# First modulation in float32 with its weights as stationary tiles, by quarters of rows; silu(c) broadcast once

## The chip, the cores and the metric

One core of a Trainium2 chip runs the whole program. The metric is the device time of one execution in microseconds, as the median of several. The engines are TensorE (PE; PEld is its load of stationary weights), VectorE (DVE), ScalarE (ACT), GpSimd (POOL) and SyncE (SP), whose queue issues nearly all transfers.

## The reference

Two blocks of a network run one behind the other; only the head of the first is touched. In layer 0, x (512 rows of 1024) and ctx (256 rows) are normalised, modulated by a vector that depends on c or c_ctx, and multiplied by w_in:

```python
mod_lat = (jax.nn.silu(c) @ w_ada[l] + b_ada[l])[:, None, :]
mod_ctx = jax.nn.silu(c_ctx) @ w_ada[l] + b_ada[l]
sh1, sc1, gt1, sh2, sc2, gt2 = jnp.split(mod_lat, 6, axis=-1)
csh1, csc1, cgt1, csh2, csc2, cgt2 = jnp.split(mod_ctx, 6, axis=-1)
h_lat = modulate(rms_norm(x_lat, g_mix[l]), sh1, sc1)   # h * (1 + scale) + shift
h_ctx = modulate(rms_norm(x_ctx, g_mix[l]), csh1, csc1)
z = h @ p['w_in']
```

The first modulation needs sh1 and sc1, the first two sixths of w_ada (1024 x 2048), for the two vectors c and c_ctx. The other four sixths are needed later in the layer, and all six again in layer 1.

## The kernel before

Activations lie with features on the partitions: 8 tiles of 128 features by 512 rows (x) and 256 rows (ctx). Large products keep float32 accuracy by splitting each operand into a rounded part and the rest (`hi`, `lo`; type float32r) and adding three products: hi by hi, hi by lo, lo by hi. `weights` does this for a weight tile of 128x1024: a copy on ScalarE (line 295) and a subtraction on VectorE or, where `pool` is set, GpSimd (line 296). `prods` issues the three matmuls of a product (line 425).

A scheduler orders the instructions of each engine by program order and by when its own model has their inputs ready; each engine then takes its instructions in that order. Tiles come from pools with a number of buffers a tag. The tag u6 has 18: the tiles of w_mod (`raw6`), the spare split weights and the split, modulated activations H all come from it. PSUM has two double banks (`psJ`) and four single ones (`psM`).

The head of `first_block` runs in this order. c and c_ctx are loaded as 16 columns (`cc`), silu is formed by a tanh and a product (lines 1344 and 1345; it leaves out the factor 0.5, which comes later), and split into `cparts`. x is loaded, then w_mod in 16 tiles of 512 KB. `stats` squares x on ScalarE (line 564), adds on VectorE, sums over partitions with a matmul by ones (line 571), takes the power -0.5 on GpSimd (line 343) and spreads the result with transposes (line 349). `modulation` runs twice, for half of the features each: for 8 k-tiles the weights are split, and the four columns of `cparts` are the stationary tile while 512 columns of weights stream (line 1382); the four rows of sums are copied out and transposed back to columns (line 1388), and lines 1395 to 1398 form shift and gain in `mods`. `second` then forms one tile of H: a scaled product on VectorE (line 1415), a rounded copy on ScalarE (line 1416), the rest on VectorE (line 1417). Three units of w_in, whose PSUM banks are kept, are multiplied in two halves of k; `silus` broadcasts silu(c) over the partitions with 16 transposes (line 555) and four copies (line 556), for the other sixths of w_ada, which VectorE multiplies (`ada_block`, line 532). Then the gates follow (`gates`), whose first matmul is of line 330. `silus` runs a second time behind the first layer's merge, since its buffers are used for other things meanwhile. `g_entry`, a product of two gains, is formed at the head in `consts` and used by `entry` for the second block.

Of the kernel before, what the change touches and what calls it, by code (L numbers as in the profile page):

```python
# [20 lines left out]
D = 1024  # L21
KD = 8
# [77 lines left out]
def _layout(inp):  # L100
# [6 lines left out]
    w = g["w_ada"][0][:, :2 * D].reshape(KD, 128, 2, 2, T)  # L107
    a["w_mod"] = np.ascontiguousarray(w.transpose(3, 0, 1, 2, 4)).reshape(2, KD, 128, 2 * T)
# [160 lines left out]
class Build:  # L269
# [782 lines left out]
    def attention(self, l, H, nq, gates, per):  # L1052
# [36 lines left out]
        for h in range(H_A):  # L1089
# [18 lines left out]
         "b0": (0.1, 0.3), "bl": (0.4, 1), "st": (0, 0, 1, 1, 2), "l": ({}, {"late": 2, "va": 0.5, "ai": 50, "aw": (0.3, 1), "bs": (0, 1), "bv": (0.1, 0.9), "bp": (0, 0.9), "bn": (0, 0.5), "as": (0, 0.7), "av": (0, 1), "ap": (0, 1)}), "ql": 0, "oa": (), "r2": ((0, 0), (1, 1)), "sg": 0, "lag": 4, "sc": (0.3, 0.8), "ve": 10, "vw": (0, 1), "bi": (29, 6, 0, 0, 0, 0, 0, 0, 0), "bw2": (0, 0.8), "mp": ((1, 2), (1, 5)), "up": (1, 1, 1), "fin": {3: (1, 1, 0), 4: (3, 1, 0), 5: (4, 2, 3), 6: (0, 1, 3), 10: (1, 1, 0)}, "pri": (0, 0, 0, 0, 0, 0, 0, 0, 200, 0, 0), "ns": (0, 0.8), "nv": (0, 1), "raw": (0, 1), "rpw": (0, 1)}  # L1108
# [230 lines left out]
    def first_block(self):  # L1339
# [4 lines left out]
        nc.scalar.activation(cc[:, 1], cc[:, 0], AF.Tanh, scale=0.5)  # L1344
        nc.vector.scalar_tensor_tensor(cc[:, 2], cc[:, 1], 1.0, cc[:, 0], op0=ALU.add, op1=ALU.mult)
# [14 lines left out]
        parts = self.cp.tile([128, KD, 2, 2], F32R, name="cparts")  # L1360
        c2 = cc[:, 2].rearrange("p (k c) -> p k c", c=2)
        nc.scalar.activation(parts[:, :, 0], c2, AF.Copy)
        nc.vector.tensor_sub(parts[:, :, 1], c2, parts[:, :, 0].bitcast(F32))
        norm, pre = {}, []
        W = self.W

        wmod = {}

        def fetch(half):
            for k in range(KD):  # L1370
                wmod[half, k] = raw6()
                nc.sync.dma_start(wmod[half, k], io["w_mod"][half, k])

        def modulation(half):

            ps = self.psJ()
            for k in range(KD):
# [11 lines left out]
            v = col[:, :32].rearrange("p (s m a c) -> p s m a c", s=2, m=4, a=2)  # L1389
            ms = slice(half * 4, half * 4 + 4)  # L1390
            out = mods[:, :, ms]
            b = self.col("b_ada0", 0, 16).rearrange("p (s m) -> p s m", s=2)[:, :, ms]
            g = self.col("g_mix0", 0, 8)[:, ms].unsqueeze(2).to_broadcast([128, 4, 2])
            for i in range(2):
                nc.vector.scalar_tensor_tensor(out[:, i], v[:, i, :, 0], 0.5, b[:, i].unsqueeze(2).to_broadcast([128, 4, 2]),
                                               op0=ALU.mult, op1=ALU.add)
            nc.vector.scalar_tensor_tensor(out, v[:, :, :, 1], 0.5, out, op0=ALU.mult, op1=ALU.add)
# [27 lines left out]
        for m in range(KD):  # L1425
            nc.sync.dma_start(X[m][:, :T], io["xT"][m])
        fetch(0)
        stats(0)
        modulation(0)
        j = self.psJ()  # L1430

        def unit(i, pool):
            pre.append(([(j[:, i * T:i * T + T] if i < 2 else self.psM(), 0, T)],
                        self.weights(io["w_in"][0, i], spare=True, pool=pool), 0))

        fetch(1)
        modulation(1)
        for i in range(3):
            unit(i, W["up"][i])
        for k in range(KD):  # L1440
            nc.sync.dma_start(X[k][:, T:], io["ctxT"][k])
        ahead = lead(0)
        for ks in (range(4), range(4, KD)):
            for _ in ks:
# [97 lines left out]
    def entry(self, X):  # L1542
# [3 lines left out]
        H, rc = S["H"], S["rc"]  # L1546

# [851 lines left out]
```

## Time and profile before

| | us |
|---|---|
| median of 3 runs | 3387.93 |
| lowest and highest | 3387.03, 3388.76 |
| profiled execution, device time | 3382.73 |
| its span | 3381.0 |

The profile is of one execution. A timeline's row gives the start in the span, the length from the first start to the last end, and the count; matmuls are pipelined, so that the distance to the next row's start is often the better price. A window's row gives the stretch, its length, the busy time and count of PE, PEld, DVE, ACT and POOL, the clock, the share of the DMA engines and GB/s; the clock is the TensorE clock that was granted, as a share of 2.4 GHz. In the windows ahead of 25 us that column reads 1.00, although a matmul of 512 columns takes 0.43 us there from start to start and 0.23 us later; in this stretch the durations tell the level.

### The profile page before, as it was taken

Reading aid. Unit: us, or ns where it says so; the run is one execution under the profiler, and the core shown is the slowest. Engines: PE = TensorE matmul, PEld = TensorE weight load, DVE = VectorE, ACT = ScalarE, POOL = GpSimd, SP = SyncE. Lnnn points to the kernel's source line nnn. Section 1 sums busy time; section 2 is a strip of 40 time slices with the busy share of each in tenths; the row PEclk is TensorE's granted clock in tenths of the full one; section 3 lists DMA queues with packets and bytes.
Section 4 is the critical chain, followed back from the end, with each engine's and each line's share of the span. In section 5 each row is a group of like instructions: output and inputs, shape, how many; then the busy total and the mean of one; then the engine's idle time right before and its main releaser. Section 6 shows DMA issues by size and latency. Waiting matters only on the chain.

```text
span 3381.0 us, 45398 instructions
## 1 busy us (share of the span) xinstructions
PE 3278.9 (97%) x17673; PEld 2789.9 (83%) x17673; DVE 2242.8 (66%) x3810; ACT 1387.4 (41%) x2393; POOL 488.1 (14%) x488
## 2 busy tenths in 40 slices
PE   7999999999999999998999999999999989999998
PEld 4888878888888887887788888988888877798887
DVE  7958788469775565667866556776555777764555
ACT  5236566232222233545634333454233435552222
POOL 2002133210000020112330000220000513420001
PEclk9999999999999999999999999999999999999999
DMA  8720113324452121221162223222323231222222
GB/s 289 260 80 34 54 35 119 124 67 129 155 162 91 64 99 65 85 71 35 56 209 75 98 95 111 74 94 78 103 94 113 82 104 45 91 91 90 94 99 75
DMA packets 105993, 337.35 MB, mean 100 GB/s; under 512 B 12529, under 2 KB 18033, under 8 KB 105777
## 3 DMA queue, kind: packets, MB, share of 16 engines
q1 hardware_dynamic: 97632, 313.34, 28.2%
q10 hardware_dynamic: 5184, 10.49, 0.8%
q0 software_dynamic: 2960, 10.62, 0.8%
q8 instruction: 139, 2.28, 0.3%
q14 instruction: 78, 0.63, 0.1%
HBM read 311.20 MB, written 23.20 MB: 99 GB/s over the span
## 4 chain that ended last, share of the span: by engine, by line
PE 44%; DVE 5%; ACT 2%; issue 2%; POOL 1%; DMA 0%; SPq 0%; ACTq 0%; POOLq 0%; DVEq 0%
PE psM L425 37%; PE psM L330 2%; DVE u L324 1%; PE psJ L959 1%; DVE t L1589 1%; PE psM L1017 1%; PE psM L2109 1%; PE psM L2070 1%; DVE t L1588 1%; DVE wlo L296 1%; PE psM L669 0%; PE psM L2101 0%; PE psM L504 0%; POOL stat L495 0%; ACT whi L295 0%
## 5 line engine op out<-in xcount | busy, mean ns | idle before, releaser
L425 PE MATMUL psM<-u,whi 128*128 128x512 f32 (+1 forms) x5312 | 1435.5, 363 | 2.5 <-ACT u L322 1.0
L425 PEld LDWEIGHTS psM<-u,whi 128*128 128x128 f32 x5312 | 928.7, 189 | 156.7 <-ACT u L322 2.5
L425 PE MATMUL psM<-u,wlo 128*128 128x512 f32 (+1 forms) x2656 | 912.6, 362 | 1.9 <-DVE wlo L296 1.9
L295 ACT ACTIVATE whi<-wraw 128x1024 fp32r<-128x1024 f32 x393 | 413.6, 1054 | 986.2 <-PE psM L425 609.5
L296 DVE TENSOR_TENSOR wlo<-wraw,whi 128x1024 fp32r<-128x1024 f32 x393 | 488.3, 1244 | 277.4 <-ACT whi L295 273.9
L425 PEld LDWEIGHTS psM<-u,wlo 128*128 128x128 f32 x2656 | 481.9, 189 | 78.7 <-DVE wlo L296 2.6
L330 PE MATMUL psM<-u,whi 128*128 128x512 f32 (+1 forms) x1610 | 428.7, 352 | 2.7 <-DVE u L320 1.3
L330 PEld LDWEIGHTS psM<-u,whi 128*128 128x128 f32 x1610 | 280.1, 190 | 45.1 <-issue 2.1
L330 PE MATMUL psM<-u,wlo 128*128 128x512 f32 (+1 forms) x805 | 280.5, 349 | 0.0
L425 PE MATMUL psM<-u,wspare 128*128 128x256 f32 (+1 forms) x1584 | 258.3, 318 | 3.9 <-DVE t L1588 3.2
L425 PE MATMUL psJ<-u,whi 128*128 128x512 f32 (+1 forms) x1184 | 256.7, 337 | 0.0
L425 PEld LDWEIGHTS psM<-u,wspare 128*128 128x128 f32 x1584 | 228.5, 197 | 20.8 <-issue 3.4
L495 POOL TENSOR_TENSOR stat<-stat,t 128x256 f32<-128x256 f32 x100 | 93.8, 952 | 975.7 <-ACT t L493 909.7
L425 PEld LDWEIGHTS psJ<-u,whi 128*128 128x128 f32 x1184 | 182.0, 188 | 26.3
L330 PEld LDWEIGHTS psM<-u,wlo 128*128 128x128 f32 x805 | 152.9, 190 | 20.4 <-DVE wlo L296 0.4
L532 DVE SCALAR_TENSOR_TENSOR silu<-araw,silu 128x1024 f32<-128x1024 f32 x128 | 156.1, 1220 | 16.0 <-DMA araw<-in_w_ada_dram 16.0
L322 ACT ACTIVATE u<-t 128x512 fp32r<-128x512 f32 (+2 forms) x114 | 77.5, 682 | 215.2 <-DVE t L1293 128.4
L425 PE MATMUL psJ<-u,wlo 128*128 128x512 f32 x592 | 154.2, 338 | 0.0
L320 DVE TENSOR_TENSOR pt<-psM,pt 128x512 fp32r<-128x512 f32 x156 | 105.9, 685 | 36.8 <-ACT pt L319 35.2
L319 ACT ACTIVATE pt<-psM 128x512 fp32r<-128x512 f32 x156 | 91.4, 595 | 88.9 <-PE psM L669 83.4
L324 DVE SCALAR_TENSOR_TENSOR u<-t,u 128x512 fp32r<-128x512 f32 (+2 forms) x114 | 88.1, 775 | 48.9 <-ACT u L322 48.8
L330 PE MATMUL psM<-whi,u 128*128 128x512 f32 (+2 forms) x356 | 112.3, 383 | 3.9 <-DVE V L640 2.5
(355 smaller groups left out, 4395.8 us busy)
## 6 DMA issues: line engine op xcount, KB each, us to landing
wraw<-in_w_up_dram SPq DMA_DIRECT2D x88, 512.0 KB, 3.5
wraw<-in_ffn_gu_dram SPq DMA_DIRECT2D x88, 512.0 KB, 3.5
araw<-in_w_ada_dram SPq DMA_DIRECT2D x80, 512.0 KB, 4.3
wraw<-in_w_in_dram SPq DMA_DIRECT2D x70, 512.0 KB, 3.5
wraw<-in_w_down_dram SPq DMA_DIRECT2D x44, 512.0 KB, 3.5
wraw<-in_ffn_dn_dram SPq DMA_DIRECT2D x44, 512.0 KB, 3.5
wraw<-in_od_in_dram SPq DMA_DIRECT2D x24, 512.0 KB, 3.5
araw<-in_w_mod_dram SPq DMA_DIRECT2D x16, 512.0 KB, 10.2
```

What stands on the lines that cost most here:

```text
L295: nc.scalar.activation(hi[:, :n], raw[:, :n], AF.Copy)
L296: (nc.gpsimd if pool else nc.vector).tensor_sub(lo[:, :n], raw[:, :n], hi[:, :n].bitcast(F32))
L319: nc.scalar.activation(hi, src, AF.Copy)
L320: (nc.gpsimd if pool else nc.vector).tensor_sub(lo, src, hi.bitcast(F32))
L322: nc.scalar.activation(hi, src, AF.Copy, scale=scale) if isinstance(scale, float) else \
L324: nc.vector.scalar_tensor_tensor(lo, src, scale, hi.bitcast(F32), op0=ALU.mult, op1=ALU.subtract)
L330: nc.tensor.matmul(out, w[a][wrows, wcols], x[b][xrows, xcols], start=first and i == 0, stop=last and i == 2)
L425: self.nc.tensor.matmul(ps[:, lo - c0:hi - c0], w[a][:, wc], x[b][:, lo:hi], start=first and i == 0 and a == b, stop=last and i == len(ks) ...
L495: (nc.vector if last == 1 else nc.gpsimd).tensor_add(st["acc"][:, c], st["acc"][:, c], s[:, c])
L532: nc.vector.scalar_tensor_tensor(self.junk, raw, 0.5, self.silu[cnd], op0=ALU.mult, op1=ALU.mult, accum_out=m)
L959: self.nc.tensor.matmul(ps[:, c0 - keys[0][0]:c1 - keys[0][0]], q[:96, x, qs:qs + 128], k[:96, y, c0:c1], start=i == 0, stop=i == 2)
L1017: nc.tensor.matmul(o, V[:, kt, i], pt[:, b], start=kt == 0 and b == 0, stop=kt == 5 and b == 1)
```

## The change

The modulation is cut into four quarters of 256 features instead of two halves. Its weights are no longer split: a 128x128 block of w_mod, in float32, is the stationary tile, and the two columns of silu(c) and silu(c_ctx) stream through it, so that the result comes out with features on the partitions and needs no transpose. w_mod is laid out anew for that. Behind each quarter the two H tiles that it allows are formed, and those parts of the three first products whose k-tiles are there are issued (`begun`): the first unit behind the first quarter, the second with the second, the third with the third. The transfers of w_mod are issued a quarter ahead, each behind a unit of w_in.

`silus` runs at the head, before `stats`; it writes the two broadcast tiles to DRAM through GpSimd's queue, and the second call loads them from there instead of forming them again. The column table `cols` is loaded behind x instead of before c; silu is formed behind that; `g_entry` is formed in `entry`. No weights of this stage are split on GpSimd any more (the entries `mp` and `up` of the table `W` go).

```diff
-    w = g["w_ada"][0][:, :2 * D].reshape(KD, 128, 2, 2, T)
-    a["w_mod"] = np.ascontiguousarray(w.transpose(3, 0, 1, 2, 4)).reshape(2, KD, 128, 2 * T)
+    w = g["w_ada"][0][:, :2 * D].reshape(4, 2, 128, 2, 4, TC)
+    a["w_mod"] = np.ascontiguousarray(w.transpose(4, 0, 2, 1, 3, 5)).reshape(4, 4, 128, 2 * T)
...
         self.junk, self.silu = new(), [new(), new()]
+        if self.silu_d:
+            for d, s in zip(self.silu_d, self.silu):
+                self.nc.sync.dma_start(s, d)
+            return
         for cnd, s in enumerate(self.silu):
...
                 self.nc.scalar.activation(s[:, half * T:half * T + T], ps, AF.Copy)
+            d = self.dp.tile([128, 1024], F32, name=f"silu{cnd}")
+            self.nc.gpsimd.dma_start(d, s)
+            self.silu_d.append(d)
...
-        def fetch(half):
+        banks = self.psJ()
+
+        def fetch(q):
+            for kp in range(4):
+                wmod[q, kp] = raw6()
+                nc.sync.dma_start(wmod[q, kp], io["w_mod"][q, kp])
+
+        def modulation(q):
+
+            ps = banks[:, q % 2 * T:q % 2 * T + 8].rearrange("p (s m c) -> p s m c", s=2, m=2)
             for k in range(KD):
-                wmod[half, k] = raw6()
-                nc.sync.dma_start(wmod[half, k], io["w_mod"][half, k])
-
-        def modulation(half):
-
-            ps = self.psJ()
-            for k in range(KD):
-                w = self.weights(None, raw=wmod[half, k], pool=(half, k) in W["mp"])
-                for a in range(2):
-                    for i in range(2):
-                        c = slice(i * T, i * T + T)
-                        nc.tensor.matmul(ps[:4, c], parts[:, k].rearrange("p a c -> p (a c)"), w[a][:, c],
-                                         start=k + a == 0, stop=k + a == KD)
-            rows = self.p4.tile([128, 1024], F32, name="rows", tag="p4", bufs=self.n4)
-            nc.scalar.activation(rows[:4], ps[:4], AF.Copy)
-            col = self.psM()
-            for j in range(8):
-                nc.tensor.transpose(col[:, 4 * j:4 * j + 4], rows[:4, j * 128:j * 128 + 128], self.ident[:4, :4])
...
+                w = wmod[q, k // 2][:, k % 2 * T:k % 2 * T + T].rearrange("p (s m f) -> p s m f", s=2, m=2)
+                for i in range(2):
+                    for m in range(2):
+                        nc.tensor.matmul(ps[:, i, m], w[:, i, m], cc[:, 2, 2 * k:2 * k + 2], start=k + i + m == 0,
+                                         stop=k == KD - 1 and i + m == 2)
...
         for m in range(KD):
             nc.sync.dma_start(X[m][:, :T], io["xT"][m])
+        self.cols = self.load("cols", [128, NCOLS])
+        nc.scalar.activation(cc[:, 1], cc[:, 0], AF.Tanh, scale=0.5)
+        nc.vector.scalar_tensor_tensor(cc[:, 2], cc[:, 1], 1.0, cc[:, 0], op0=ALU.add, op1=ALU.mult)
+        self.silus()
+        j = self.psJ()
...
+        def begun(u, q):
+
+            self.run_all(self.prods([pre[u]], H, [slice(0, T)], (2 * q, 2 * q + 1), not q, q == 3))
+
         fetch(0)
         stats(0)
...
         ahead = lead(0)
...
+        for q in range(4):
+            if q < 3:
+                unit(q)
+                fetch(q + 1)
+            else:
+                for k in range(KD):
+                    nc.sync.dma_start(X[k][:, T:], io["ctxT"][k])
+            modulation(q)
+            for _ in range(2):
                 next(ahead)
-            if ks[0]:
+            if q == 3:
                 stats(1)
-            for u in pre:
-                self.run_all(self.prods([u], H, [slice(0, T)], ks, not ks[0], bool(ks[0])))
-        self.silus()
+            for u in range(min(q + 1, 3)):
+                for p in range(q + 1) if u == q else (q,):
+                    begun(u, p)
...
+        g_entry = self.cp.tile([128, 8], F32, name="g_entry")
+        nc.vector.tensor_mul(g_entry, self.col("g_final", 0, 8), self.col("ln_mix_pre0", 0, 8))
```

## Rows read from the trace of the kernel before

**Rows 1.** The page: busy us of each engine (share of the span) and instructions.

```profile
PE 3278.9 (97%) x17673; PEld 2789.9 (83%) x17673; DVE 2242.8 (66%) x3810; ACT 1387.4 (41%) x2393; POOL 488.1 (14%) x488
```

**Rows 2.** Windows of the start: stretch, length, engines' busy us, clock, DMA share, GB/s.

```profile
30.00:35.00 5.00, 2.98 (x11) 0.76 (x10) 4.93 (x10) 3.98 (x5) 2.80 (x1) 0.92 1.03 400
...
45.00:50.00 5.00, 2.49 (x5) 1.55 (x6) 5.00 (x5) 1.67 (x3) 3.01 (x2) 0.50 0.56 194
50.00:55.00 5.00, 5.00 (x14) 3.86 (x13) 5.00 (x8) 3.76 (x7) 0.00 (x0) 0.53 1.01 332
55.00:60.00 5.00, 5.00 (x24) 4.14 (x23) 5.00 (x8) 3.92 (x9) 0.00 (x0) 1.00 0.42 146
```

**Rows 3.** Windows of the stretches behind the start, same columns.

```profile
100.00:200.00 100.00, 100.00 (x566) 88.03 (x565) 81.10 (x175) 22.45 (x36) 0.00 (x0) 1.00 0.61 202
...
400.00:500.00 100.00, 94.56 (x550) 79.21 (x549) 76.25 (x163) 63.08 (x140) 32.72 (x36) 1.00 0.12 40
```

**Rows 4.** TensorE's timeline of the start: start, us, instruction, count, [idle before].

```profile
12.12 3.57 PE L571 MATMUL psM<-ones,t 128*128 128x1 f32 x16 [12.12 <-DVE t L566]
...
17.98 1.11 PE L349 MATMUL psM<-c_ident,sm 128*128 128x128 f32 x4 [0.98 <-POOL sm L343]
...
20.17 1.05 PE L1382 MATMUL psJ<-wlo,cparts 128*4 128x512 f32 x2
21.02 1.05 PE L1382 MATMUL psJ<-whi,cparts 128*4 128x512 f32 x2
...
25.14 0.63 PE L1382 MATMUL psJ<-whi,cparts 128*4 128x512 f32 x2
...
48.62 8.31 PE L425 MATMUL psJ<-u,wspare 128*128 128x512 f32 x23 [2.51 <-DVE u L1417]
...
59.26 5.60 PE L425 MATMUL psJ<-u,wspare 128*128 128x512 f32 x24
64.70 0.95 PE L571 MATMUL psM<-ones,t 128*128 128x1 f32 x8
...
69.25 1.04 PE L555 MATMUL psM<-c_ident,ccol 128*128 128x128 f32 x8
...
71.51 0.74 PE L330 MATMUL psM<-u,whi 128*128 128x512 f32 x2
```

**Rows 5.** Groups by form, 10 to 72 us: count, busy us, mean ns, idle.

```profile
L296 DVE TENSOR_TENSOR wlo<-araw,whi 128x1024 fp32r<-128x1024 f32 x14 | 18.3, 1338 | 4.4 <-ACT whi L295 2.9 <-issue 1.4
...
L1417 DVE SCALAR_TENSOR_TENSOR u<-t,mods,u 128x512 fp32r<-128x512 f32 x8 | 7.7, 1012 | 0.0
...
L1415 DVE SCALAR_TENSOR_TENSOR t<-t,mods,psM 128x512 f32<-128x512 f32 x8 | 5.6, 737 | 0.0
L1416 ACT ACTIVATE u<-t,mods 128x512 fp32r<-128x512 f32 x8 | 5.3, 708 | 4.6 <-DVE t L1415 4.6
```

**Rows 6.** TensorE's timeline around the second broadcast of silu(c).

```profile
703.72 1.03 PE L555 MATMUL psM<-c_ident,ccol 128*128 128x128 f32 x8
704.51 0.48 PE L425 MATMUL psJ<-u,wspare 128*128 128x256 f32 x2
...
706.75 0.65 PE L555 MATMUL psM<-c_ident,ccol 128*128 128x128 f32 x4 [0.25 <-ACT silu L556]
...
707.82 1.85 PE L504 MATMUL psM<-ones,t 128*128 128x1 f32 x16
```

**Rows 7.** Windows behind two trains of one-column passes, columns as in rows 2.

```profile
709.00:710.00 1.00, 1.00 (x11) 1.00 (x11) 0.29 (x2) 0.00 (x0) 0.05 (x1) 1.00 0.63 254
710.00:711.00 1.00, 1.00 (x7) 1.00 (x6) 1.00 (x3) 0.00 (x0) 1.00 (x1) 0.51 0.00 0
...
713.00:714.00 1.00, 1.00 (x9) 1.00 (x8) 1.00 (x4) 0.12 (x1) 0.00 (x0) 0.78 0.00 0
...
2304.00:2306.00 2.00, 2.00 (x12) 2.00 (x12) 0.16 (x1) 0.00 (x0) 1.02 (x1) 0.51 0.86 337
```

**Rows 8.** TensorE's timeline: the second of these trains.

```profile
2303.17 1.10 PE L504 MATMUL psM<-ones,stat 128*128 128x1 f32 x8 [0.48 <-DVE stat L495]
```

More of the change, by code (lines that the diff above doesn't have):

```diff
@@ L1343, in first_block @@
         nc.sync.dma_start(cc[:, 0], io["ccol"])
-        nc.scalar.activation(cc[:, 1], cc[:, 0], AF.Tanh, scale=0.5)
-        nc.vector.scalar_tensor_tensor(cc[:, 2], cc[:, 1], 1.0, cc[:, 0], op0=ALU.add, op1=ALU.mult)
         X = [self.t3() for _ in range(KD)]
@@ L1359, in first_block @@
         mods = self.cp.tile([128, 2, KD, 2], F32, name="mods")
[L1360 to L1363, printed above, removed]
         norm, pre = {}, []
-        W = self.W
         wmod = {}
-        def fetch(half):
-            for k in range(KD):
-                wmod[half, k] = raw6()
-                nc.sync.dma_start(wmod[half, k], io["w_mod"][half, k])
@@ new lines, in fetch @@
+        def fetch(q):
[4 more added lines that the diff above has]
+            ps = banks[:, q % 2 * T:q % 2 * T + 8].rearrange("p (s m c) -> p s m c", s=2, m=2)
+            for k in range(KD):
+                w = wmod[q, k // 2][:, k % 2 * T:k % 2 * T + T].rearrange("p (s m f) -> p s m f", s=2, m=2)
[3 more added lines that the diff above has]
+                                         stop=k == KD - 1 and i + m == 2)
+            ms = slice(q * 2, q * 2 + 2)
@@ L1391, in modulation @@
             out = mods[:, :, ms]
             b = self.col("b_ada0", 0, 16).rearrange("p (s m) -> p s m", s=2)[:, :, ms]
-            g = self.col("g_mix0", 0, 8)[:, ms].unsqueeze(2).to_broadcast([128, 4, 2])
+            g = self.col("g_mix0", 0, 8)[:, ms].unsqueeze(2).to_broadcast([128, 2, 2])
             for i in range(2):
-                nc.vector.scalar_tensor_tensor(out[:, i], v[:, i, :, 0], 0.5, b[:, i].unsqueeze(2).to_broadcast([128, 4, 2]),
+                nc.vector.scalar_tensor_tensor(out[:, i], ps[:, i], 0.5, b[:, i].unsqueeze(2).to_broadcast([128, 2, 2]),
@@ L1396, in modulation @@
                                                op0=ALU.mult, op1=ALU.add)
-            nc.vector.scalar_tensor_tensor(out, v[:, :, :, 1], 0.5, out, op0=ALU.mult, op1=ALU.add)
             nc.vector.scalar_tensor_tensor(out[:, 1], out[:, 1], 1.0, g, op0=ALU.add, op1=ALU.mult)
@@ L1426, in first_block, with unit @@
             nc.sync.dma_start(X[m][:, :T], io["xT"][m])
+        self.cols = self.load("cols", [128, NCOLS])
[3 more added lines that the diff above has]
+        j = self.psJ()
+        def unit(i):
+            pre.append(([(j[:, i * T:i * T + T] if i < 2 else self.psM(), 0, T)],
+                        self.weights(io["w_in"][0, i], spare=True), 0))
+        def begun(u, q):
+            self.run_all(self.prods([pre[u]], H, [slice(0, T)], (2 * q, 2 * q + 1), not q, q == 3))
         fetch(0)
         stats(0)
[L1429 to L1441, printed above, removed]
-        ahead = lead(0)
-        for ks in (range(4), range(4, KD)):
-            for _ in ks:
+        ahead = lead(0)
+        for q in range(4):
[7 more added lines that the diff above has]
+            for _ in range(2):
                 next(ahead)
-            if ks[0]:
+            if q == 3:
                 stats(1)
-            for u in pre:
-                self.run_all(self.prods([u], H, [slice(0, T)], ks, not ks[0], bool(ks[0])))
-        self.silus()
+            for u in range(min(q + 1, 3)):
+                for p in range(q + 1) if u == q else (q,):
+                    begun(u, p)
         lat, ctx, A, B = slice(0, T), slice(T, TJ), slice(0, TC), slice(TC, T)
@@ L1546, in entry @@
         H, rc = S["H"], S["rc"]
+        g_entry = self.cp.tile([128, 8], F32, name="g_entry")
+        nc.vector.tensor_mul(g_entry, self.col("g_final", 0, 8), self.col("ln_mix_pre0", 0, 8))
         def take(m, c, last):
-            self.split(H[m], X[m][:, c], c=c, scale=self.g_entry[:, m:m + 1])
+            self.split(H[m], X[m][:, c], c=c, scale=g_entry[:, m:m + 1])
             self.square(st, X[m][:, c], c, last)
@@ L2339, in load @@
             return t
-        self.cols = load("cols", [128, NCOLS])
         self.ident = load("ident", [128, 128])
@@ L2348, in consts @@
         self.mod = [[self.cp.tile([128, 48], F32, name=f"mod{c}{l}") for l in range(L)] for c in range(2)]
-        self.g_entry = self.cp.tile([128, 8], F32, name="g_entry")
-        nc.vector.tensor_mul(self.g_entry, self.col("g_final", 0, 8), self.col("ln_mix_pre0", 0, 8))
     def run(self):
@@ L2361, in run @@
             self.joint, self.bank_i, self.side, self.tail, self.ahead = True, -1, None, iter(()), []
-            self.pn, self.odd = None, False
+            self.pn, self.odd, self.silu_d = None, False, []
             with tc.tile_pool(name="pm", bufs=1, space=PSUM) as self.pm, contextlib.ExitStack() as self.pairs, \
```

4 lines of the change are left out of this document (1 added, 3 removed).

## The prediction

> **What bounds the kernel now.** I read the page's engine totals first: TensorE is busy 97% of the span [rows 1]. Then the windows over the rest of the trace, to see whether a shift of the start would be taken up later: from 100 to 200 us TensorE is busy all of the time, and the emptiest stretch before 700 us still has 94.6 of 100 us [rows 3]. So nothing downstream waits for the start to get out of its way, and a microsecond gained or lost before the gates begin is a microsecond of the span. As the marker I take the first matmul of the gates, line 330, at 71.51 us [rows 4]: what the change does to the start is how far this matmul moves. Everything TensorE does before it I read from the timeline, and its granted clock from the windows of the start [rows 2].
>
> In the timeline the reader is to see four things. TensorE does nothing until 12.12 us, when the squares of x are summed. The old modulation streams 512 columns a matmul, two of them 0.85 us apart from the next two at 20.17 (the lower of the two clock levels, 1.2 GHz), and two in 0.63 us at 25.14 (2.4 GHz). The first products come at 48.62, after both halves of the modulation: 23 of them take 8.31 us, a good part of that at a clock of 0.50 to 0.53, and from 55 us on the clock is whole and a product takes 0.23 us (24 in 5.60). And between 30 and 50 us TensorE is far from full (2.98 of 5 us, then 2.49 of 5) [rows 2, 4]: it waits for the split of the modulation's weights, 1.34 us a tile on VectorE (line 296) behind a copy on ScalarE [rows 5]. This slack is what the change can win.
>
> **The change, part by part.** *Removed:* 16 splits of w_mod (a copy on ScalarE and 1.34 us on VectorE each, two of them on GpSimd [rows 5]), the 64 matmuls of 512 columns, 16 small transposes, two PSUM copies. They bound the start before; after, they are simply gone.
>
> *Added: the modulation in float32.* Each quarter multiplies 8 k-tiles by 4 blocks of 128 columns: 32 matmuls with a 128x128 float32 stationary tile and two moving columns. The nearest row is line 571, a float32 stationary tile with one moving column: 8 matmuls there are 16 records, so a matmul is two passes, and 16 passes took 3.57 us at 12.12, that is 0.223 us a pass; the 8 passes at 64.70, under the full clock, took 0.95 us, 0.119 a pass [rows 4]. (Line 504, of the same form, has 16 passes in 1.85 us at 707.82 [rows 6].) So a quarter is 64 passes: 14.3 us at the lower level, 7.6 at the upper. All four, 256 passes: 57.1 or 30.5 us. A second moving column I price at nothing; the load of 128 stationary columns makes the pass.
>
> *Which level?* This decides the case. The start is at the lower level (0.223 at 12.12), so the first quarter is. What do trains of such passes do to a full clock? At 707.82 sixteen one-column passes run in a stretch where TensorE has next to no idle time, after eight transposes and a few products; one microsecond reads 1.00, the next one (710 to 711) reads 0.51, and only in 713 to 714 (0.78), after products, does it come back [rows 6, 7]. At 2303.17 a train of eight passes behind 0.48 us of idle is followed by 0.51 in the stretch from 2304 on [rows 7, 8]. After such a fall dense products needed from about 3 us (710 to 713) to 6 us (48.62 to about 55) to get the full clock back [rows 2, 4, 7]. A quarter here is a train of 64 passes, four times as long as those. I therefore take the lower level for all four quarters: 57.1 us. Both ends stay for the range.
>
> The Trainium skill, page "TensorE: Matmul & The Clock Gate", section "Why this matters for your kernels", advises keeping TensorE busy without gaps to have the full clock; by it a train without gaps would end at the upper level, which is the second rival below. The trace here speaks against it for trains of this form [rows 6, 7, 8].
>
> *Moved: the products by quarter.* Their number stays 72 (6, 18, 30 and 18 by quarter). They ran in 48.62 to 69.25 with the clock recovering; now they come in bursts between quarters. The bursts of 6 and 18 follow a train, so I price them at 0.43 us (half of 0.85 [rows 4]): 10.3 us. The last 48 come nearly together: 14 at 0.43 until the clock is back, 34 at 0.227 (line 425 at 59.26: 24 in 5.45 us start to start): 13.7 us. Together 24.0; bounds 16.3 (all at 0.227) and 31 (all at 0.43).
>
> *Moved: the broadcast of silu(c)* to before 12 us. Its 16 transposes (0.28 us each by the four at 17.98 [rows 4]) need only c and the identity, two small transfers at the head of SP's queue; TensorE is idle there until 12.12, which is the cover. Four ScalarE copies of 0.6 us go between the squares; if they delay the last square that costs up to 1.5 us; I take nothing, since x is issued earlier by the move of the column table behind it. Its old place cost TensorE 2.3 us (69.25 to 71.51), which goes.
>
> *Kept in DRAM.* Two 0.5 MB writes on GpSimd's queue, about 2.6 us of all DMA engines at the 400 GB/s of [rows 2]: hidden, because a quarter of w_mod is 2.1 MB, 5.2 us at that rate, against 14.3 us of TensorE. In front of GpSimd's power for the first rstd they could stand only if queued before it; they are ready well ahead of it. If the TensorE cover were gone, 2.6 us would show. The second broadcast near 704 us becomes two loads on SP's queue, where little else is issued; TensorE saves 16 transposes (eight take 0.79 us start to start, from 703.72 to 704.51, so 1.6 us) and 0.25 us of idle [rows 6]: 1.9 us. The fall of the clock at 710 may go with it, another 1.6 us (3.2 us at half); the sixteen one-column passes behind it stay, so I take nothing.
>
> *Tiles.* Weights, spare tiles and H share 18 buffers: the fourth quarter's four tiles can be fetched only when the second quarter has been multiplied (about 45 us), and are needed about 60: hidden at the lower clock, by some 10 us. g_entry and the column table: small operations off TensorE, nothing.
>
> **The sum.** TensorE starts at 12.1; row sums 3.6; broadcast of rstd 1.1; modulation 57.1; products 24.0; sums for ctx 0.95 and their two transposes 0.4 (at most 0.28 each, by the four at 17.98) [rows 4]: the gates begin at 99.3 instead of 71.5, 27.8 us later. Less the second broadcast: 25.9 us. The profiled execution took 3382.73, so 3408.6 in its terms; the median of the runs shown is 5.2 us above it, which I carry: **3414 us**, 0.8% slower. About 0.2%, 6.8 us, is what a measurement of this kernel can tell from no change.
>
> **The rivals.**
>
> *Rival 1, queue order.* TensorE takes its instructions in order. If the order has each quarter's products right behind its modulation, TensorE waits for the H tiles: two small VectorE steps, then lines 1415, 1416 and 1417 (0.74, 0.71, 1.01 us), the second tile behind the first: some 3.3 us a quarter [rows 5], up to 10 for three quarters, since VectorE and ScalarE have little else. Against it: a quarter's weights are there early, so the next quarter can be queued in the gap. End: +36 us, 3424.
>
> *Rival 2, the other side: the clock holds.* If the trains run at 0.119 a pass from the first quarter on and the products at 0.227, the sum is 12.1 + 4.7 + 30.5 + 16.3 + 1.4 = 65.0, 6.5 us earlier; with the 1.9 near 704 the time is 3379.5, 0.25% faster. It decides from an average pass of 0.15 us: (71.5 + 1.9 - 12.1 - 4.7 - 16.3 - 1.4) / 256. For it: passes of this form are at 0.119 right behind products [rows 4, 6]. Against it: what they do after that [rows 7, 8].
>
> *Rival 3, mixed.* The products between quarters bring the clock back often enough that a third to two thirds of the passes are at 0.119: 9 to 18 us less, and some of the products' 7.7 too: +2 to +15 us, about 3396.
>
> The Trainium skill, same page, section "LDWEIGHTS (loading the stationary operand)", gives columns divided by 1.2 in ns, an estimate of 107 ns for 128, whatever the clock; 256 of them would be 27 us and the time near 3380. The measured passes are 0.119 and 0.223 [rows 4], so it falls under rival 2.
>
> **How the numbers follow.** Forecast 0.66, rival 1 0.14, rival 3 0.10, rival 2 0.10. The forecast's own bounds: products at 16.3 and some passes fast, +13; products all slow and part of rival 1's waits, +38. The range 3398 to 3426 (+10 to +38) holds the forecast, rival 1 but for its edge, and the upper part of rival 3: about 0.82. Slower by over 0.2%: forecast, rival 1 and some 0.04 of rival 3, 0.84; within 0.2%: the rest of rival 3 and a little of rival 2, 0.08; faster 0.08.
>
> **What would show it.** In the changed profile: 64 records a quarter under the new modulation's line, at 0.22 us each; windows with a clock near 0.5 through most of 24 to 85 us; the gates' first matmul near 99 us; TensorE without long idle from 12 us on (with 3 us gaps ahead of the products: rival 1); no transposes of c near 704. I am wrong if passes of two columns are at 0.12 us with a whole clock, if a matmul takes another number of passes than two, or if the products ride through on the full clock between the quarters.

## The result, and the profile after

| | before | after |
|---|---|---|
| median of 4 runs each, same chip | 3387.57 us | 3408.01 us |
| lowest to highest | 3387.03 to 3388.76 | 3403.06 to 3410.14 |
| profiled execution, its span | 3382.73, 3381.0 | 3403.06, 3401.3 |

The changed kernel is slower. The medians differ by 20.4 us. The ratio on record is 1.0065, with a 95% interval of 1.0054 to 1.0077, that is 18 to 26 us (it is not formed from these two medians, whose own ratio is 1.0060). The profiled executions differ by 20.3 us, so the two traces can be set against each other directly.

The page of the changed kernel, engine totals (against [rows 1]):

```profile
PE 3304.4 (97%) x17833; PEld 2827.4 (83%) x17833; DVE 2225.3 (65%) x3802; ACT 1368.4 (40%) x2370; POOL 474.7 (14%) x485
```

TensorE has 25.5 us more work, VectorE and ScalarE some 18 us less each. TensorE is the engine that has none to spare. Its timeline of the start, which answers to [rows 4] (start, length, instruction, count, idle before):

```profile
3.34 3.67 PE L559 MATMUL psM<-c_ident,ccol 128*128 128x128 f32 x16 [3.34 <-DVE ccol L1421]
14.56 4.43 PE L1381 MATMUL psJ<-ccol,araw 128*128 128x2 f32 x20 [7.55 <-DMA araw<-in_w_mod_dram]
18.85 3.55 PE L578 MATMUL psM<-ones,t 128*128 128x1 f32 x16
22.27 9.53 PE L1381 MATMUL psJ<-ccol,araw 128*128 128x2 f32 x44
31.65 1.09 PE L349 MATMUL psM<-c_ident,sm 128*128 128x128 f32 x4
32.54 6.83 PE L1381 MATMUL psJ<-ccol,araw 128*128 128x2 f32 x32
39.23 2.91 PE L425 MATMUL psJ<-u,wspare 128*128 128x512 f32 x6
41.93 6.82 PE L1381 MATMUL psJ<-ccol,araw 128*128 128x2 f32 x32
49.07 6.99 PE L1381 MATMUL psJ<-ccol,araw 128*128 128x2 f32 x32 [0.32 <-DVE mods L1388]
55.92 6.50 PE L425 MATMUL psJ<-u,wspare 128*128 128x512 f32 x18
62.25 3.63 PE L1381 MATMUL psJ<-ccol,araw 128*128 128x2 f32 x32
65.74 3.01 PE L425 MATMUL psM<-u,wspare 128*128 128x512 f32 x12
...
69.05 1.62 PE L1381 MATMUL psJ<-ccol,araw 128*128 128x2 f32 x14
70.52 2.76 PE L425 MATMUL psJ<-u,wspare 128*128 128x512 f32 x11
...
74.26 7.67 PE L1381 MATMUL psJ<-ccol,araw 128*128 128x2 f32 x50
84.03 0.79 PE L425 MATMUL psJ<-u,wspare 128*128 128x512 f32 x1 [2.10 <-ACT u L1408]
...
91.42 1.02 PE L578 MATMUL psM<-ones,t 128*128 128x1 f32 x8 [1.29 <-DVE t L573]
94.46 0.59 PE L349 MATMUL psM<-c_ident,sm 128*128 128x128 f32 x2 [2.01 <-POOL sm L343]
94.70 1.20 PE L330 MATMUL psM<-u,whi 128*128 128x512 f32 x2
```

The gates' first matmul (line 330) stands at 94.70 us instead of 71.51: 23.2 us later. The new modulation is line 1381, and its counts add up to 256 records, two for each of the 128 matmuls. Start to start, 32 passes took 6.69 us from 32.54 (0.209 each), 44 took 9.38 from 22.27 (0.213), but 32 took only 3.49 from 62.25 (0.109) and 14 took 1.47 from 69.05. These are the two levels of the clock. The full one came back within the 18 products at 55.92 (0.35 us each, between the two levels), and was lost again inside the last 50 passes, as the windows show (columns as in [rows 2]; the first line is for later):

```profile
5.00:10.00 5.00, 2.01 (x10) 1.61 (x8) 1.38 (x2) 4.65 (x10) 1.29 (x2) 1.00 0.98 310
...
65.00:70.00 5.00, 5.00 (x32) 4.41 (x32) 3.21 (x7) 1.80 (x3) 0.00 (x0) 1.00 0.00 0
70.00:75.00 5.00, 5.00 (x30) 4.35 (x30) 0.00 (x0) 0.00 (x0) 0.00 (x0) 1.00 0.00 0
75.00:80.00 5.00, 5.00 (x36) 5.00 (x36) 0.00 (x0) 0.00 (x0) 0.00 (x0) 0.75 0.71 213
80.00:85.00 5.00, 2.90 (x12) 2.53 (x12) 2.78 (x7) 1.74 (x4) 0.00 (x0) 0.50 0.00 0
```

From 75 to 80 us TensorE is busy all of the time, and yet the clock falls. (In this stretch the windows up to 60 us read 1.00, as those ahead of 25 us did before; there the pitch of the passes, 0.21 us, tells the level.)

Behind the start the difference is 24.7 us from 100 to 300 us. It is 27.1 at the row sums ahead of layer 1 and 26.0 at the first run of 512-column products behind them (718.51 before, 744.48 after). One row of each kernel shows the first of these, before and after in this order:

```profile
695.03 0.95 PE L504 MATMUL psM<-ones,t 128*128 128x1 f32 x8
```

```profile
722.12 0.95 PE L504 MATMUL psM<-ones,t 128*128 128x1 f32 x8
```

So the second broadcast gave back 1.1 us net. Its transposes are gone, but a wait of 1.02 us of TensorE for GpSimd (740.15) has come, which the trace of before does not have there. Later the difference wanders between 29.5 and 20.3 us, and the clock falls in other places: behind this stretch it stands at half for 65 us in before and for 49 us in after, which is worth up to 8 us. Here is the same work at the same place in the trace of before and in that of after:

```profile
2154.54 6.42 PE L425 MATMUL psM<-u,wspare 128*128 128x256 f32 x29
```

```profile
2178.85 3.72 PE L425 MATMUL psM<-u,wspare 128*128 128x256 f32 x29
```

The 29 products stood at a clock of 0.50 in before and 1.00 in after, and 2.7 us of the start's loss were gone by it. No step of the change touches the code of these products. Executions of one kernel differ among themselves in this way: those of the kernel before ran from 3374 to 3391 us on the several chips of this study.

### The profile page after: what moved, and what is told of

It reads as the page before. It is cut to its first block, busy times and chain, and to the rows that moved or that the text cites. A ratio compares the mean times of both kernels' runs of the same rounds, so it can differ in the third digit from the quotient of the medians.

```text
span 3401.3 us, 45687 instructions
## 1 busy us (share of the span) xinstructions
PE 3304.4 (97%) x17833; PEld 2827.4 (83%) x17833; DVE 2225.3 (65%) x3802; ACT 1368.4 (40%) x2370; POOL 474.7 (14%) x485
## 3 DMA queue, kind: packets, MB, share of 16 engines
q1 hardware_dynamic: 97920, 314.38, 27.9%
q0 software_dynamic: 3248, 11.67, 0.9%
## 4 chain that ended last, share of the span: by engine, by line
PE 44%; DVE 5%; ACT 2%; issue 1%; POOL 1%; DMA 0%; SPq 0%; POOLq 0%; ACTq 0%; DVEq 0%
PE psM L425 37%; PE psM L330 2%; PE psJ L966 1%; DVE u L324 1%; DVE t L1591 1%; PE psM L1024 1%; PE psM L2111 1%; PE psM L2072 1%; DVE wlo L296 1%; DVE t L1590 0%; PE psM L676 0%; PE psM L2103 0%; POOL stat L495 0%; PE psM L504 0%; POOL sm L343 0%
## 5 line engine op out<-in xcount | busy, mean ns | idle before, releaser
L330 PEld LDWEIGHTS psM<-u,wlo 128*128 128x128 f32 x805 | 152.7, 190 | 20.3 <-DVE wlo L296 0.4
```

Source lines behind the costliest of these rows:

```text
L330: nc.tensor.matmul(out, w[a][wrows, wcols], x[b][xrows, xcols], start=first and i == 0, stop=last and i == 2)
```

## The experiments

Each ratio is against executions of the kernel before on the same chip. The runs without an interval are single executions, of which the trace is what counts, above all the start of the gates' first matmul (94.70 after, 71.51 before). This marker scatters by itself: the first two runs are the kernel before up to the gates, and there it stands at 72.59 and 74.05. A shift of some 2.5 us or less in one trace shows nothing.

**Do thin passes bring a full clock down? (two runs)** Into the gates of the kernel before, where TensorE is full and its clock 1.00, go 32 float32 matmuls with a 128x128 stationary tile and two moving columns, 64 passes, a quarter of the new modulation. Its control has 31 products of 512 columns at the same place, which take the same time at a full clock. The added results are not used.

```diff
         for i, (j, pieces) in enumerate(jobs):
             yield from part(i, j, pieces, pre[i][0][0][0] if i < len(pre) else None)
+            if l == 0 and i == 9:
+                ps = self.psM()
+                for t in range(32):
+                    nc.tensor.matmul(ps[:, 2 * t:2 * t + 2], self.ident, self.cc[:, 2, 0:2], start=True, stop=True)
# the control instead
+                for t in range(31):
+                    nc.tensor.matmul(ps, H[0][:, 0, :128], H[0][:, 1, :T], start=True, stop=True)
```

> The kernel before, with 32 float32 matmuls added (stationary: the identity; two moving columns; result unused) in the dense stretch of the first layer's gates. That is a train of 64 passes, as long as one quarter of the changed modulation. Theory (such a train costs the clock its upper level): the train's first passes are at 0.11 us each, the later ones at 0.21, so the train lasts 9 to 12 us; the granted clock reads near 0.5 within the train, and products behind it run at 0.43 us a piece for some us more. Rival (a pass costs the same at any clock, the start was slow only because TensorE had been idle before): all 64 passes at 0.11, 7 us, the clock stays at 1.00 and the products behind it at 0.23 us.

> The control to the train: the kernel before with 31 products of 512 columns added at the same place (split tiles of H as both operands; result unused), 7.0 us at the full clock. Both theories: 7.0 us, clock 1.00 throughout. If the clock falls here too, it is the insertion and not the form of the matmul that costs it.

The train and what follows it, in TensorE's timeline and in the windows:

```profile
106.38 10.56 PE L623 MATMUL psM<-ccol,c_ident 128*128 128x2 f32 x64
116.81 1.20 PE L330 MATMUL psM<-u,whi 128*128 128x512 f32 x2
```

```profile
106.00:108.00 2.00, 2.00 (x21) 2.00 (x19) 1.97 (x4) 1.33 (x2) 0.00 (x0) 1.00 0.79 217
...
110.00:112.00 2.00, 2.00 (x11) 2.00 (x11) 1.97 (x6) 0.00 (x0) 0.00 (x0) 0.50 0.92 307
...
118.00:120.00 2.00, 2.00 (x7) 1.52 (x6) 0.46 (x2) 0.00 (x0) 0.00 (x0) 0.50 0.73 225
120.00:122.00 2.00, 2.00 (x10) 1.66 (x9) 0.00 (x0) 0.00 (x0) 0.00 (x0) 1.00 0.13 53
```

The control, timeline and one of its windows (all of them read 1.00):

```profile
107.82 7.22 PE L623 MATMUL psM<-u 128*128 128x512 f32 x31
114.87 0.62 PE L330 MATMUL psM<-u,whi 128*128 128x512 f32 x2
```

```profile
112.00:114.00 2.00, 2.00 (x11) 1.65 (x10) 1.97 (x4) 0.00 (x0) 0.00 (x0) 1.00 0.95 362
```

TensorE is busy 2.00 of 2.00 us in all of these windows, in both kernels. The train takes 10.43 us to the next row, the control 7.05. The first passes of the train run at 0.109 us, the others at 0.21, and the products behind it stay at half until 120 us (two in 0.99 us at 116.81, against 0.46 at 114.87 in the control). So the train itself lowers the clock, without idle time, and the work behind it pays too. The control's operands are of another type (float32r), but that is not it: the wide float32 passes of the exchanged operands, below, keep the full clock. Whether the few moving columns or the load of a stationary tile for each of them does it was not separated.

**Do TensorE's passes set the start?** Every second k-tile of the new modulation is left out, that is half of its sum.

```diff
-            for k in range(KD):
+            for k in range(0, KD, 2):
```

> The changed kernel with every second k-tile left out of the first modulation's sums (all of w_mod is still loaded): 128 passes instead of 256. Theory (TensorE's passes set the start): the gates' first matmul, at 94.7 us in the changed kernel, comes 20 to 27 us earlier, near 70 to 75. Rival (the transfers of w_mod, the buffers they wait for, or the waits for H set it): less than 10 us earlier, with TensorE idle in front of the quarters instead.

```profile
70.02 0.71 PE L330 MATMUL psM<-u,whi 128*128 128x512 f32 x2
```

The gates begin at 70.02 us, 24.7 earlier than in the changed kernel, and the time of the one execution is 3379.89 us. Half of the 46.66 us that the changed kernel's passes took is 23.3, and the modulation began 1.2 us earlier (13.32). The transfers and the H tiles were the same. The passes, with the clock that they leave behind, set the start.

**The same modulation with the operands exchanged.** The two columns of silu become the stationary tile, and the float32 weights, still unsplit, stream 512 columns a pass; the two rows of sums are copied out and transposed back. This is 64 passes instead of 256.

```diff
-                w = wmod[q, k // 2][:, k % 2 * T:k % 2 * T + T].rearrange("p (s m f) -> p s m f", s=2, m=2)
-                for i in range(2):
-                    for m in range(2):
-                        nc.tensor.matmul(ps[:, i, m], w[:, i, m], cc[:, 2, 2 * k:2 * k + 2], ...)
+                nc.tensor.matmul(ps[:2], cc[:, 2, 2 * k:2 * k + 2], wmod[q, k // 2][:, k % 2 * T:k % 2 * T + T],
+                                 start=k == 0, stop=k == KD - 1)
+            rows = self.p4.tile([128, 1024], F32, name="rows", tag="p4", bufs=self.n4)
+            nc.scalar.activation(rows[:2, :T], ps[:2], AF.Copy)
+            col = self.psM()
+            for t in range(4):
+                nc.tensor.transpose(col[:, 2 * t:2 * t + 2], rows[:2, t * 128:t * 128 + 128], self.ident[:2, :2])
```

> The changed kernel with the operands of its modulation exchanged: the two columns of silu are the stationary tile, and 512 columns of unsplit float32 weights stream through it; the two rows of sums are copied out and transposed to columns. One matmul for each k-tile and quarter, two passes each, 0.85 us at the full clock by line 2185 of the kernel before: 27 us for all, which is what 256 passes cost at the full clock too. Theory (the form of the passes costs the clock, not their sum of time at the full clock): once the clock is up, near 25 us, it stays at 1.00; the modulation takes 28 to 33 us instead of 46, the products 0.23 us each, and the gates begin between 72 and 84 us instead of 94.7; the time falls by 10 to 22 us against the changed kernel. Rival (float32 passes cost the clock in any form, or the start is bound by something else): the gates begin later than 88 us.

From its timeline:

```profile
44.53 4.15 PE L425 MATMUL psJ<-u,wspare 128*128 128x512 f32 x17
48.61 3.59 PE L1378 MATMUL psJ<-araw,ccol 128*2 128x512 f32 x8
52.14 0.41 PE L1384 MATMUL psM<-c_ident,rows 2*128 2x2 f32 x4
...
59.54 6.17 PE L1378 MATMUL psJ<-araw,ccol 128*2 128x512 f32 x14
...
68.91 0.50 PE L425 MATMUL psJ<-u,wspare 128*128 128x512 f32 x1 [2.06 <-ACT u L1411]
...
78.02 0.43 PE L349 MATMUL psM<-c_ident,sm 128*128 128x128 f32 x2 [2.01 <-POOL sm L343]
78.21 0.71 PE L330 MATMUL psM<-u,whi 128*128 128x512 f32 x2
```

Eight passes take 3.53 us at the full clock (0.44 each), so 64 take 28.2 us; 256 thin ones at 0.109 would take 27.9. At the same level the two forms cost TensorE the same. The wide one keeps the level: the 17 products at 44.53, between two stretches of it, take 0.24 us each. The gates begin at 78.21, 16.5 us earlier than after the change, although the waits of 2.06 and 2.01 us are still there. Timed: 3384.68 us against 3383.17, ratio 1.0006 (0.9997 to 1.0016). The interval is -1 to +5 us: most of the loss of 20 us, or all of it, is gone by the choice of the moving operand. In the trace the gates still begin 4.2 to 6.7 us later than in the three traces with the start of the kernel before, and nothing is won.

**The broadcast of silu, early and kept, alone** (the kernel before with `silus` at the head, written to DRAM on GpSimd's queue as in the change).

```diff
+        self.silus()
         fetch(0)
         stats(0)
         modulation(0)
...
-        self.silus()
```

> The kernel before with one part of the change alone: silu(c) broadcast at the head, written to DRAM through GpSimd's queue and loaded again for the second use. Theory A (as the prediction priced it): the gates' first matmul comes 2.3 us earlier than 71.5, and some 1 to 2 us more are saved near 704 us; the time falls by 3 to 4 us, which is hardly more than the scatter of the runs. Theory B (the two writes of 0.5 MB run beside the first tiles of w_mod, and hold them back): the first tile of w_mod is used some 2 us later than in the kernel before, and the gates' first matmul moves by less than 1 us; the time stays.

Ratio 1.0002 (0.9992 to 1.0011), gates at 70.55, 1.0 us earlier, which is within the marker's scatter. At the head the squares come later: ScalarE ends the last at 14.15 us instead of 11.67, with the four copies of silu among them, which the prediction had named and priced at nothing. The first split of w_mod begins 0.3 us later (12.56 against 12.27), not the 2 us of theory B. Near 704 us this trace shows no saving: it is 1.4 us behind that of before ahead of this place, and 1.6 behind it after. This part neither costs nor wins anything measurable.

**The silu tiles written later** (the changed kernel, with the two writes on SP's queue behind the transfers of the start).

```diff
-            self.nc.gpsimd.dma_start(d, s)      # in silus, right behind the copies
+        for cnd, s in enumerate(self.silu):     # behind the last begun(u, p)
+            nc.sync.dma_start(d, s)
```

> The changed kernel with the two writes of silu to DRAM issued on SP's queue behind the transfers of the start, instead of at 6 to 8 us on GpSimd's. Theory (they hold back the first tiles of w_mod, and TensorE starts the modulation at 14.6 instead of 12.3 for it): the modulation starts at 12 to 13 us and the gates' first matmul comes about 2 us earlier than 94.7, up to what another place of the clock's steps adds or takes (some 3 us). Rival (w_mod came later for another reason): it starts after 14 us.

```profile
12.60 4.43 PE L1378 MATMUL psJ<-ccol,araw 128*128 128x2 f32 x20 [5.38 <-DMA araw<-in_w_mod_dram]
...
61.48 4.58 PE L1378 MATMUL psJ<-ccol,araw 128*128 128x2 f32 x32
65.92 5.23 PE L425 MATMUL psM<-u,wspare 128*128 128x512 f32 x12
```

The modulation begins at 12.60 instead of 14.56. The size is uncertain: with the early writes it began at 14.56, 14.40, 13.59 and 13.32 in four traces (the changed kernel, the exchanged operands, the sums for ctx earlier, half of k), with late ones at 12.60 and 12.22 (here and in the first of the three attempts). So the writes had held back the first tile of w_mod by 0.7 to 2.3 us. Yet the gates begin at 95.65, 1 us later than with the early writes, and the time is 3408.08 us. The 12 products at 65.92, which took 2.85 us to the next row of their form in the changed kernel, now took 5.07, because the clock fell at another place of work in the same order. A gain of 2 us at the head of such a stretch is within what the clock does to it.

**The sums for ctx earlier** (the changed kernel; transfers and row sums of ctx ahead of the third quarter).

```diff
-            else:
+            if q == 2:
                 for k in range(KD):
                     nc.sync.dma_start(X[k][:, T:], io["ctxT"][k])
+                stats(1)
             modulation(q)
...
-            if q == 3:
-                stats(1)
```

> The changed kernel with the transfers and the row sums of ctx issued ahead of the third quarter instead of behind the fourth. Theory (the waits ahead of the gates, 1.29 us for VectorE and 2.01 us for GpSimd, are the sums of ctx come late): the gates' first matmul comes 3 to 4 us earlier than 94.7, the matmuls by ones and their wait move between quarters. Rival (they only show where the last products' stall would stand anyway): less than 1 us.

```profile
38.25 2.91 PE L425 MATMUL psJ<-u,wspare 128*128 128x512 f32 x6
40.96 3.74 PE L1381 MATMUL psJ<-ccol,araw 128*128 128x2 f32 x32
...
61.40 13.61 PE L1381 MATMUL psJ<-ccol,araw 128*128 128x2 f32 x64 [0.32 <-DVE mods L1388]
77.02 1.84 PE L578 MATMUL psM<-ones,t 128*128 128x1 f32 x8 [2.01 <-DVE t L573]
```

Gates at 93.73, 1.0 us earlier where 3 to 4 were expected, and 3408.05 us; the modulation too had begun 1.0 us earlier (13.59). The scheduler now put the products of the third quarter behind the last train, so that 64 passes run without a product between them, 0.213 us each, and the waits for the sums moved with them. The expectation failed; what the exposed sums cost by themselves wasn't isolated. The first two rows show something else: behind the burst of six products, which took 2.71 us to the next row as in the changed kernel (2.70), the 32 passes ran at the full clock, where they had taken 0.21 us each in the changed kernel.

**Products by half alone** (the kernel before, with split weights; the first products of the first half are issued ahead of the second half of the modulation).

```diff
-        modulation(1)
         for i in range(3):
             unit(i, W["up"][i])
...
         for ks in (range(4), range(4, KD)):
+            if ks[0]:
+                modulation(1)
+                for k in range(KD):
+                    nc.sync.dma_start(X[k][:, T:], io["ctxT"][k])
             for _ in ks:
                 next(ahead)
```

> The kernel before, split weights and halves as they were, with one part of the change alone: the first products' first half of k issued behind the first half of the modulation instead of behind both. Theory (in the kernel before TensorE waited from 30 to 48 us for VectorE, and that was what there was to win): 36 of the 72 products move into that stretch, and the gates begin 5 to 10 us earlier than 71.5; the time falls by as much. Rival (VectorE, not the order of TensorE, sets the start: it is busy up to 56 us with splits and H): the gates move by less than 3 us, because H's first tiles then stand in front of the second half's splits on VectorE.

Ratio 1.0046 (1.0029 to 1.0063), gates at 80.67. Both readings that I had written down fell. TensorE's timeline and ScalarE's show where the time goes:

```profile
37.36 0.80 PE L425 MATMUL psJ<-u,wspare 128*128 128x512 f32 x1 [7.71 <-ACT u L1416]
```

```profile
35.64 1.06 ACT L295 ACTIVATE wspare<-wraw 128x1024 fp32r<-128x1024 f32 x1 [0.23 <-DMA wraw<-in_w_in_dram]
36.60 2.54 ACT L1416 ACTIVATE u<-t,mods 128x512 fp32r<-128x512 f32 x4
52.18 4.85 ACT L295 ACTIVATE whi<-araw 128x1024 fp32r<-128x1024 f32 x5 [13.04 <-issue]
```

TensorE waits 7.71 us for the first copy for H (line 1416), which stands in ScalarE's order behind the splits of w_in, and these wait for their transfers. Then TensorE multiplies the 36 products. ScalarE meanwhile stands idle for 13.04 us, and the second half's splits go on only at 52.18, when TensorE has turned to that half (51.47). The profile names no releaser for this wait. The likely one, not tested, are the three buffers of `whi`, which come free with the modulation's matmuls, and these now stand behind the products. So with split weights this order delayed the modulation; the exchanged operands above ran the same order of quarters with unsplit weights and began their gates at 78.21.

**Three attempts at a version faster than before.** First, the exchanged operands with the sums of ctx earlier and the silu tiles written later. Second, the kernel before with the early broadcast written later. Third, the second plus three w_mod tiles of the second half streamed unsplit against four stationary columns (two of them zero), and the splits of the three units on VectorE. From the edit of the third:

```diff
+                if (half, k) in W["mp"]:
+                    for i in range(2):
+                        c = slice(i * T, i * T + T)
+                        nc.tensor.matmul(ps[:4, c], whole[:, k].rearrange("p a c -> p (a c)"), wmod[half, k][:, c],
+                                         start=False, stop=False)
+                    continue
-"mp": ((1, 2), (1, 5)), "up": (1, 1, 1)
+"mp": ((1, 2), (1, 5), (1, 6)), "up": (0, 0, 0)
```

> The version with exchanged operands (two stationary columns, 512 float32 columns streaming), with the sums of ctx ahead of the third quarter and the writes of silu behind the transfers of the start. Theory: the modulation starts at 12 to 13 us, the waits of 2 us in front of the gates go, and the gates begin near 74 to 76 us instead of 78.2; the time is 2 to 5 us below the kernel before, hardly more than the scatter. Rival (moving the sums of ctx changes TensorE's order as it did in the changed kernel, so that the products come late): the gates begin at 78 us or later and the time is that of the kernel before.

> The kernel before with silu(c) broadcast at the head and kept, but written to DRAM behind the transfers of the start. Theory (the writes beside the first tiles of w_mod ate what the move of the transposes gave): the modulation starts at 12.3 to 12.8 us instead of 13.7, the gates' first matmul comes 2 to 3 us earlier than 71.5, and the time falls by 2 to 4 us, 0.1%. Rival (VectorE sets the start, TensorE's transposes were beside it): less than 1 us at the gates.

> As the run with silu kept and written late, and besides three of the second half's eight w_mod tiles are not split: they stream as float32, two passes each, against four stationary columns of which two are zero; the three first units are split on VectorE instead of GpSimd. Theory (VectorE and GpSimd bound the start before, TensorE had slack from 30 to 48 us): the second half of the modulation ends 2 to 3 us earlier than 41.3, no small VectorE step takes 2 us beside GpSimd any more, the first long run of products starts near 44 instead of 48.6, and the gates begin at 63 to 67 us; the time falls by 5 to 9 us. Rival (the transfers of w_mod, which end near 32 us, and VectorE's H tiles bound it): the gates begin later than 68 us.

The first: 3385.29 us against 3380.6, ratio 1.0017 (1.0008 to 1.0025). Its modulation begins at 12.22. The marker, 66.86, can't be compared here, since 18 of the first products now stand behind it; TensorE waits for ctx's H tiles inside the gates:

```profile
80.28 0.38 PE L330 MATMUL psM<-u,whi 128*128 128x256 f32 x1 [3.05 <-DVE u L1409]
```

The second: ratio 1.0011 (1.0001 to 1.0020), gates at 71.62. The modulation begins at 13.51, not at the 12.3 to 12.8 expected. What became of the time taken off TensorE at the end isn't shown. The last split of the modulation holds TensorE, as it does for 2.23 and 2.21 us in the first two runs, which have the start of the kernel before:

```profile
44.27 0.63 PE L1386 MATMUL psJ<-wlo,cparts 128*4 128x512 f32 x2 [2.21 <-DVE wlo L296]
```

The third: ratio 0.9999 (0.9990 to 1.0008), gates at 68.35, 3.2 us earlier than in before, outside the 63 to 67 expected; in the time this can't be seen. The long run of products began at 47.93, where 44 was expected and before has 48.62. No version beat the kernel before by what a measurement can tell.

## Why the prediction came out as it did

The time of 3408.0 us lies 6 us below the forecast of 3414 and inside the range; the sign is as forecast. The mechanism was the one named: trains of thin passes run at the lower clock, and TensorE's passes set the start. The train with its control shows the first, the halved modulation the second, and the exchanged operands that most or all of the lost time comes back with the clock. The terms of the sum, against what the timeline of the changed kernel measured (start to start):

| term | forecast | measured |
|---|---|---|
| TensorE starts | 12.1 | 14.56 |
| row sums | 3.6 | 3.42 |
| broadcast of rstd | 1.1 | 0.89 |
| modulation, 256 passes | 57.1 | 46.66 |
| products, 72 | 24.0 | 22.18 |
| waits for modulated tiles and `mods` | 0 | 2.42 |
| sums for ctx, transposes, waits | 1.4 | 4.56 |
| gates' first matmul | 99.3 | 94.70 |

The 4.6 us between the sums are what is left of 12.6 us that the forecast had too much and 8.0 us that it had too little; that most of it cancels is luck.

*Modulation, mis-sized by 10.4 us.* The step that failed is "I therefore take the lower level for all four quarters". Some 74 of the 256 passes ran at 0.109 us: 32, 14 and, worked out from 7.67 us for the last 50, 28 more. That is 74 x (0.223 - 0.109) = 8.4 us. The other 2.0 are the pitch, 0.212 for 182 passes where the row sums had given 0.223 by the length of their row; from start to start (12.12 to 15.55 [rows 4]) they give 0.214. The prediction had what it needed for the first: it read that dense products bring the clock back within 3 to 6 us, and itself priced the burst of 18 at 7.7 us, longer than that. So the train behind that burst was to begin at the full clock, as it did. The length of a burst alone doesn't settle it: the burst of 6 lasted 2.70 us and the passes behind it stayed at 0.21, but in the run with the sums for ctx earlier they ran at the full clock behind the same burst. One of the prediction's own signs of being wrong showed as well: the 30 products from 65.74 to 74.26 rode through at the full clock, 0.235 us each. With 29% of its passes fast the case lies between the forecast and rival 3, which began at a third; the result lies nearer the forecast.

*Start, 2.4 us late.* "Kept in DRAM: hidden" failed. The cover that it named, a quarter's 14.3 us on TensorE, lies behind the first tile's arrival; at 6.40 us, when the first write was issued, the DMA engines were busy (0.98 in the window 5 to 10 us), and from 7.01 us TensorE had nothing to do. Writing later gave back 2.0 us of it in one pair of traces, 0.7 to 2.3 over all pairs; what is left lies within the scatter of the start, 12.12 to 13.24 us in three traces of the kernel before.

*Sums for ctx, 3.2 us over.* Before, they stood at 64.70, ahead of products that covered their chain over VectorE and GpSimd [rows 4]. Now they come last, and 1.29 and 2.01 us of it are idle time. The sum had taken only TensorE's own part.

*Rival 1* was refused for the right reason: only the fourth quarter, with no next train to fill the gap, waited long (2.10 us, and 0.32 at 49.07). *Rival 2* fell for this form of pass: TensorE was without gaps and the clock did not hold. The Trainium skill, page "TensorE: Matmul & The Clock Gate", section "Why this matters for your kernels", advises a TensorE kept busy without gaps for the full clock; the trace disagrees for thin passes (2.00 of 2.00 us busy, clock 0.50) and agrees for wide ones (1.00 in the control).

*Second broadcast:* forecast 1.9 us, measured 27.1 - 26.0 = 1.1 net of the new wait of 1.02.

*Behind the start* the prediction let nothing change. The difference went from 23.2 us at the gates to 24.7 (the clock was at half for their first 3 us) and, by falls of the clock elsewhere, to 20.3. As far as the rows show, that part isn't of the change, so the closeness of 20.3 and the forecast's 25.9 holds some luck.

## What to carry to other kernels

Of a matmul with a large and a thin operand, stream the large one: at the full clock stationary tiles with few moving columns cost the same here, but a train of them takes the clock down, and what follows pays as well. Price such a train by the level that it leads to, and for each burst of dense work between trains price both levels: behind the long burst here the next train began at the full clock, behind the short one it did so in one execution and not in another. A write put on a queue that is free still shares the DMA engines with the first tiles that an idle TensorE waits for (0.7 to 2.3 us here).

## What the runs showed of the hardware

A TensorE that is busy without a gap does not by itself keep its clock: 64 passes with two moving columns took it to 0.50 and 10.43 us, 31 products of 512 columns in the same place left it at 1.00 and took 7.05 us. The pitch of a pass with a 128x128 float32 stationary tile followed the clock, 0.109 and 0.212 us, although it streams next to nothing. A float32 pass of 512 columns took 0.44 us at the full clock, about twice the 0.227 of a float32r product. And the places where the clock falls differ between executions of equal work. The times go with it: of 13 executions of the kernel before on one chip the fastest (3374 us) had a mean granted clock of 0.990, the slowest (3388 us) 0.986.
